# Half of the first output group's PSUM tiles move from ScalarE to VectorE, in a one-core hybrid decoder layer

## The chip, the cores and the metric

The kernel runs on one core of a Trainium2 chip. Its time is the device time of one execution in microseconds (us); the figure to be predicted is the median of a few executions. The core's engines are called PE (TensorE, the matrix products), DVE (VectorE), ACT (ScalarE), POOL (GpSimd) and SP (SyncE, which here only issues DMAs). Each engine works through its own list of instructions in order: an instruction that waits holds up everything behind it on its engine, and nothing on the others until they need its result.

## The reference

One layer of a decoder, sequence length 1024, model width 1024, all in float32:

```
x = x + 0.5 * swiglu(rms_norm(x))
x = x + concat(o_gdn, o_ssm) @ w_out      # the mixer
x = x + 0.5 * swiglu(rms_norm(x))
out = rms_norm(x)
```

The mixer projects the normalised input with one matrix and runs two kinds of heads over it. `o_gdn` comes from 8 heads of a gated delta rule (causal, in chunks, with a triangular solve in each chunk and a state that passes from chunk to chunk), each head normalised and gated. `o_ssm` comes from 16 state-space heads, gated by `silu(z)` and then normalised in two groups of 512 channels. The 2048 columns of both go through `w_out` (2048 x 1024). The normalisation of `o_ssm` is a factor for each token and group, so it can be applied after the product with `w_out`.

## The kernel before, in words

A matrix product in float32 precision is made of three passes: each operand is split into a high and a low part (`hi` by a ScalarE cast or scaling, `lo` by a VectorE subtraction), and `mm3` (lines 122 to 125) issues hi*hi, lo*hi and hi*lo, one product of 128x512 each. So a group of product rows in the profile always shows L123, L124 and L125 in turn.

The program runs in stages: first feed-forward block, gates and input projection, the state-space heads, the eight delta-rule heads, the output projection, second feed-forward block, final norm. The change touches the border between the last delta-rule head (head 7) and the output projection.

The output projection of the state-space part is cut into four groups (`n` = 0 to 3) of 256 columns of `o_ssm`. For each group `group_prep(n)` (line 1204) loads 256 rows of `w_out` and the group's slice of `o_ssm` by DMA, and splits both: `whi` (ACT, L138) and `wlo` (DVE, L139) are the weights, the tiles `mtt` (ACT, L1200 and DVE, L1201) the activations. `group_tile(n, b, dh)` (line 1211) then makes one output tile for token block `b` (0 to 7) and half `dh` (0 or 1) of the output columns: six products into one PSUM tile `ps_pj`, of which there are three in rotation. The tile is taken out of PSUM by one instruction: for group 0 a scaling that writes into the SBUF tile `xa` (L1220), for groups 1 to 3 a scaled addition onto `xa` on VectorE (L1222). Call the sixteen tiles of group 0 T0 to T15, in the order in which they are made: b = 0 with dh = 0, b = 0 with dh = 1, and so on. T0, T2, ... have dh = 0 and T1, T3, ... have dh = 1. The list `moved` holds their sixteen evictions, so `moved[4]` is that of T4 and `moved[5]` that of T5.

A tile's first product needs a free PSUM tile of the three, so T3 waits for the eviction of T0, T6 for T3 and so on.

Group 0 is made early: its operands come through other buffers (`out_start`, line 1228; there the weights are called `w`), and its tiles fill PE while heads 6 and 7 go through their serial parts. The serial parts that meet it are:

- head 6: its triangular solve, which runs from a chain of 62 small VectorE steps (`ft`, `fx`, L1496 and L1498) through DMAs, a VectorE transpose (`lv`, L1510) and small products with copies between them (L1516 to L1544), and then its recurrence over eight token blocks (L1554, L1556, L1559, L1561, L1565, L1568, L1573);
- head 7: `k_part` (line 1337) transposes the keys into two PSUM tiles `ps_mx` (L1346). For each of eight blocks ACT squares and sums a block (`jd`, L1350) and then DVE scales the same block (`kd`, L1352). Blocks of one PSUM tile take turns: each `kd` follows its `jd`, and the next `jd` follows that `kd`. When four blocks are read, the PSUM tile is free for the products of keys with keys and queries (`pg`, L1443 and L1444).

The order of instructions on each engine is set by a scheduler when the program is built. It ranks instructions by the order of the source and by its own estimate of when each could run. `with tc.issue_after(ins):` adds to that: instructions created inside the block on the engine of `ins` are queued behind `ins`. Line 1454 uses it to queue ACT's part of `group_prep(1)` behind T5's eviction. It binds only the engine on which that eviction runs.

Of the kernel before, what the change touches and what calls it, by code (L numbers as in the profile page):

```python
# [16 lines left out]
ALU = mybir.AluOpType  # L17
# [27 lines left out]
def kernel(  # L45
# [7 lines left out]
    V, A, G, T = nc.vector, nc.scalar, nc.gpsimd, nc.tensor  # L53
# [9 lines left out]
    def psum(tag):  # L63
        return ps.tile([P, 512], F32, name="ps_" + tag, tag=tag, bufs=PS_BUFS[tag])
# [57 lines left out]
    def mm3(o, wh, wl, mh, ml, first, last):  # L122
        T.matmul(o, lhsT=wh, rhs=mh, start=first, stop=False)  # L123
        T.matmul(o, lhsT=wh, rhs=ml, start=False, stop=False)  # L124
        return T.matmul(o, lhsT=wl, rhs=mh, start=False, stop=last)  # L125
# [759 lines left out]
    with tc.tile_pool(name="gtmp", bufs=1, side="right", reuse_waits="tile") as tp:  # L885
# [48 lines left out]
        for c in (15, 13, 11, 9, 7, 5, 3):  # L934
# [9 lines left out]
                               op0=ALU.mult, op1=ALU.mult)  # L944
# [259 lines left out]
    def group_prep(n):  # L1204

        w = load_rows_w(wp, w_out[0], (4 + n) * 256, "")
        m = out_bufs[1][n % 2 * 2:n % 2 * 2 + 2]
        ssm_prep(n, *m)
        return w, m

    def group_tile(n, b, dh, w, m):
        bs = slice(b * P, (b + 1) * P)
        ds = slice(dh * 512, (dh + 1) * 512)
        p = psum("pj")
        for j in range(2):
            last = mm3(p, m[0][:, j, bs], m[1][:, j, bs], w[0][:, j, ds], w[1][:, j, ds], j == 0, j == 1)
        o = out_bufs[0][b // 2][:, b % 2, ds]
        r = rstd_g[n // 2][:, b:b + 1]
        if n == 0:
            moved.append(A.mul(out=o, in_=p, mul=r))  # L1220
        else:
            V.scalar_tensor_tensor(out=o, in0=p, scalar=r, in1=o, op0=ALU.mult, op1=ALU.add)  # L1222
        return last

    FIRST_TILES = 4
    out_bufs, ready0, moved = [], [], []
# [107 lines left out]
    with ExitStack() as cg:  # L1334
# [37 lines left out]
        for h in range(GH):  # L1372
# [25 lines left out]
            else:  # L1398
# [15 lines left out]
                if h < GH - 1:  # L1414
                    conv_from(pre, 16 + h, vt_)
                    A.activation(out=zc, in_=zc, func=AF.Silu)
                    A.activation(out=vt_, in_=vt_, func=AF.Silu)
                else:
                    out_start()
                    for b in range(FIRST_TILES):  # L1420
                        for dh in range(2):
                            tile_end = group_tile(0, b, dh, *ready0[0])
                    tk, br2, kd = k_part(h, kt)
                    qe, dt = decays(h)
                    conv_from(pre, 16 + h, vt_)
                    A.activation(out=zc, in_=zc, func=AF.Silu)
                    A.activation(out=vt_, in_=vt_, func=AF.Silu)
# [9 lines left out]
            for b0 in range(0, NB, 2):  # L1437
# [8 lines left out]
                for i in range(2):  # L1446
                    V.scalar_tensor_tensor(out=u[:, b0 + i], in0=pg[:, i * 256:i * 256 + P],
                                           scalar=br2[:, b0 + i:b0 + i + 1], in1=dt[:, b0 + i],
                                           op0=ALU.mult, op1=ALU.mult)
                V.tensor_tensor(out=dt[:, b2],  # L1450
                                in0=pg.rearrange("p (i c) -> p i c", i=2)[:, :, P:2 * P],
                                in1=dt[:, b2], op=ALU.mult)
            if h == GH - 1:
                with tc.issue_after(moved[5].ins):
                    ready1 = group_prep(1)
            fs_u = dram.tile([4, NB, 32, 32], F32, name="fs_u", bufs=2)
            for j in range(4):
# [14 lines left out]
                            op0=ALU.mult, op1=ALU.add)  # L1472
# [20 lines left out]
            for j in range(31):  # L1493
                r, n = j // 4 + 1, 31 - j
# [46 lines left out]
            for b in range(NB):  # L1541
# [3 lines left out]
                            scalar1=-1.0, scalar2=None, op0=ALU.mult)  # L1545
# [90 lines left out]
    for n in range(4):  # L1636
        cur = ready
        for b in range(NB):

            if n == 0 and b < FIRST_TILES:  # L1640
                if b == 2:
                    ready = ready1
                continue
            if b == 2 and n < 3:
                ready = group_prep(n + 1)
                if n == 1:
                    loaded = out_load(0)
            elif b == 2:
                pair_prep(0, 0, ms[0], loaded)
                loaded = out_load(1)  # L1650
                wa = out_w(0, 0)
            for dh in range(2):
                group_tile(n, b, dh, *cur)
# [104 lines left out]
```

## Time and profile before

| | |
|---|---|
| median of 3 runs | 2297.78 us (2296.7 to 2298.23) |
| the profiled execution, its own time | 2296.6 us |
| its span, first to last instruction | 2294.9 us |
| granted TensorE clock over the span | 0.998 |
| busy: PE, DVE, ACT | 98%, 76%, 51% of the span |
| where the change lies | 1420 to 1600 us; the sixteen evictions L1220 start between 1423.4 and 1461.3 us |

In rows of the timeline the first number is the start in us from the beginning of the span, the second the length, then engine, line, operation, output<-inputs, shapes and how often; the bracket says how long the engine was idle before and whose end it waited for. Successive instructions of one engine overlap by about 0.1 us, so the distance between two starts is a little less than a length. In rows by windows the columns are the stretch, its length, and the busy time with the number of instructions of PE, PEld (weight loads), DVE, ACT and POOL, then the granted clock, the share of the DMA engines and GB/s. In rows of waits the numbers are the total in us, how often, and the longest.

### The profile page before, as it was taken

The page shows a single profiled execution, that of the slowest core. Times are in us where ns is not written, and L with a number is a line of the kernel's source. Part 1 is how long each engine was busy: PE and PEld are TensorE (multiplying, and loading weights), DVE is VectorE, ACT ScalarE, POOL GpSimd, SP SyncE. Part 2 cuts the span into 40 slices and gives each one's busy share as a digit, 9 for nine tenths or more (in the row PEclk, how much of TensorE's full clock was granted, in tenths as well). Part 3 has the DMA queues.
Part 4 walks back from the last instruction along what each step waited for, and adds up shares of the span by engine and source line. Part 5 has one row for each costly group of instructions (what it writes and reads, how often), then busy time and mean ns, then how long its engine had stood idle before and what let it go on. Part 6 is the DMA issues. An engine that isn't in the chain of part 4 may idle for free.

```text
span 2294.9 us, 31984 instructions
## 1 busy us (share of the span) xinstructions
PE 2257.9 (98%) x11654; PEld 1842.1 (80%) x11654; DVE 1751.5 (76%) x3225; ACT 1178.9 (51%) x2276; POOL 52.1 (2%) x118
## 2 busy tenths in 40 slices
PE   7999999999999999999999999999999999999998
PEld 5788888888878878888887777788878888888886
DVE  7989987769776887667667777778688676766787
ACT  7444433354366986875755566523543333334344
POOL 0000000000000110100000000000000000000000
PEclk9999999999999999999999999999999999999999
DMA  3467663497654433242356566436123232329446
GB/s 112 137 217 256 230 214 114 166 333 228 206 180 137 134 120 101 74 132 65 84 158 183 166 175 195 136 99 220 65 88 133 92 119 88 120 89 347 143 151 215
DMA packets 262194, 356.96 MB, mean 156 GB/s; under 512 B 60808, under 2 KB 167404, under 8 KB 260244
## 3 DMA queue, kind: packets, MB, share of 16 engines
q1 hardware_dynamic: 261220, 352.20, 47.2%
q0 software_dynamic: 816, 2.72, 0.3%
q8 instruction: 91, 1.49, 0.3%
q14 instruction: 67, 0.55, 0.1%
HBM read 249.34 MB, written 105.52 MB: 155 GB/s over the span
## 4 chain that ended last, share of the span: by engine, by line
PE 87%; ACT 6%; DVE 5%; issue 1%; DMA 1%; POOL 0%; SPq 0%; DVEq 0%; POOLq 0%; ACTq 0%
PE ps_pj L125 7%; PE ps_pj L123 7%; PE ps_pj L124 7%; PE ps_pj L335 6%; PE ps_pj L334 6%; PE ps_pj L336 6%; PE ps_mx L334 3%; PE ps_mx L336 3%; PE ps_mx L335 3%; PE ps_pj L564 2%; PE ps_pj L565 2%; PE ps_pj L563 2%; PE ps_pj L1260 2%; PE ps_oo L335 2%; PE ps_pj L1261 2%; PE ps_oo L334 2%
## 5 line engine op out<-in xcount | busy, mean ns | idle before, releaser
L336 PE MATMUL ps_pj<-bh,al 128*128 128x512 f32 x688 | 268.1, 390 | 0.0
L335 PE MATMUL ps_pj<-bl,ah 128*128 128x512 f32 x688 | 267.9, 389 | 0.0
L334 PE MATMUL ps_pj<-bh,ah 128*128 128x512 f32 x688 | 267.7, 390 | 0.0
L123 PE MATMUL ps_pj<-hhi,whi 128*128 128x512 f32 x576 | 229.4, 398 | 0.4 <-ACT gsb L901 0.4
L125 PE MATMUL ps_pj<-hhi,wlo 128*128 128x512 f32 x576 | 229.4, 398 | 0.0
L124 PE MATMUL ps_pj<-hlo,whi 128*128 128x512 f32 x576 | 228.3, 396 | 0.0
L336 PEld LDWEIGHTS ps_pj<-bh,al 128*128 128x128 f32 x688 | 129.2, 188 | 26.7
L335 PEld LDWEIGHTS ps_pj<-bl,ah 128*128 128x128 f32 x688 | 129.2, 188 | 26.6
L334 PEld LDWEIGHTS ps_pj<-bh,ah 128*128 128x128 f32 x688 | 129.0, 188 | 26.7
L317 DVE TENSOR_TENSOR as<-wst 128x512 f32<-128x512 f32 x220 | 144.3, 685 | 2.1 <-DMA wst<-in_ffn_w_up_dram 2.0
L241 ACT CAST hid<-hraw 128x1024 fp32r<-128x1024 f32 (+1 forms) x84 | 82.2, 980 | 123.9 <-PE ps_oo L565 46.3
L241 ACT CAST ah<-wst 128x512 fp32r<-128x512 f32 x88 | 54.5, 621 | 176.4 <-PE ps_oo L335 113.4
L242 DVE TENSOR_TENSOR al<-as,ah 128x512 fp32r<-128x512 f32 x220 | 141.1, 685 | 4.8 <-ACT ah L241 4.3
L334 PE MATMUL ps_mx<-bh,ah 128*128 128x512 f32 x352 | 138.6, 396 | 3.9 <-ACT m L343 1.3
L335 PE MATMUL ps_mx<-bl,ah 128*128 128x512 f32 x352 | 138.3, 393 | 0.5 <-DVE bl L242 0.5
L336 PE MATMUL ps_mx<-bh,al 128*128 128x512 f32 x352 | 137.8, 391 | 0.3 <-DVE al L242 0.3
L241 ACT CAST ah<-as 128x512 fp32r<-128x512 f32 x220 | 125.1, 618 | 24.1 <-DVE as L317 24.1
L125 PEld LDWEIGHTS ps_pj<-hhi,wlo 128*128 128x128 f32 x576 | 108.3, 188 | 21.9 <-issue 0.9
L123 PEld LDWEIGHTS ps_pj<-hhi,whi 128*128 128x128 f32 x576 | 108.4, 188 | 21.8 <-ACT gsb L901 0.8
L124 PEld LDWEIGHTS ps_pj<-hlo,whi 128*128 128x128 f32 x576 | 108.4, 188 | 21.1 <-issue 0.8
L242 DVE TENSOR_TENSOR hid<-hraw,hid 128x1024 fp32r<-128x1024 f32 (+1 forms) x84 | 95.0, 1131 | 26.3 <-ACT hid L241 26.1
L343 ACT COPY m<-ps_pj 128x512 f32<-128x512 f32 x88 | 51.4, 587 | 111.7 <-PE ps_pj L336 111.4
(505 smaller groups left out, 5635.4 us busy)
## 6 DMA issues: line engine op xcount, KB each, us to landing
hraw<-hid_scr SPq DMA_DIRECT2D x70, 512.0 KB, 3.9
wu_scr<-wunit SPq DMA_DIRECT2D x112, 256.0 KB, 3.6
wunits<-wu_scr SPq DMA_DIRECT2D x56, 512.0 KB, 3.8
hid_scr<-hs SPq DMA_DIRECT2D x110, 256.0 KB, 2.9
wst<-in_ffn_w_down_dram SPq DMA_DIRECT2D x50, 512.0 KB, 4.7
wst<-in_ffn_w_gate_dram SPq DMA_DIRECT2D x22, 1024.0 KB, 6.0
wst<-in_ffn_w_up_dram SPq DMA_DIRECT2D x22, 1024.0 KB, 6.0
hid_scr<-sg SPq DMA_DIRECT2D x44, 256.0 KB, 2.0
```

Source lines behind the costliest of these rows:

```text
L123: T.matmul(o, lhsT=wh, rhs=mh, start=first, stop=False)
L124: T.matmul(o, lhsT=wh, rhs=ml, start=False, stop=False)
L125: return T.matmul(o, lhsT=wl, rhs=mh, start=False, stop=last)
L241: return (A.copy(out=hi, in_=src), V.tensor_tensor(out=lo, in0=src, in1=hi.bitcast(F32), op=ALU.subtract))
L242: V.tensor_tensor(out=lo, in0=src, in1=hi.bitcast(F32), op=ALU.subtract))
L317: V.tensor_tensor(out=t, in0=v[0], in1=v[1], op=v[2])
L334: T.matmul(bank, lhsT=wh[:, k], rhs=bh[:, k], start=a, stop=False, skip_group_check=True)
L335: T.matmul(bank, lhsT=wh[:, k], rhs=bl[:, k], start=False, stop=False, skip_group_check=True)
L336: T.matmul(bank, lhsT=wl[:, k], rhs=bh[:, k], start=False, stop=z, skip_group_check=True)
L343: A.copy(out=t, in_=bank)
L563: T.matmul(bank, lhsT=hh, rhs=wh, start=first and k == 0, stop=False, skip_group_check=True)
L564: T.matmul(bank, lhsT=hh, rhs=wl, start=False, stop=False, skip_group_check=True)
```

## The change: eviction of T1, T3, ... by VectorE, and a second queueing rule

Two places change. In `group_tile` the eviction of group 0's tiles with dh = 1 is a VectorE scaling; those with dh = 0 stay on ScalarE. Where `group_prep(1)` is created, its ACT instructions are queued behind `moved[4]` (now the ACT one of the two) and its DVE instructions behind `moved[5]` (now on DVE). Before, only its ACT instructions were bound.

```diff
         if n == 0:
-            moved.append(A.mul(out=o, in_=p, mul=r))
+            if dh == 0:
+                moved.append(A.mul(out=o, in_=p, mul=r))
+            else:
+                moved.append(V.tensor_scalar(out=o, in0=p, scalar1=r, scalar2=None, op0=ALU.mult))
...
             if h == GH - 1:
-                with tc.issue_after(moved[5].ins):
+                with tc.issue_after(moved[4].ins), tc.issue_after(moved[5].ins):
                     ready1 = group_prep(1)
```

The scheduler also moves other instructions. In the changed program line numbers above 1220 are one to three higher (L1220 is L1221 on ACT and L1223 on DVE, L1352 is L1355, L1516 is L1519).

ACT, from T0's eviction (`xa`) to the second weight cast of group 1 (`whi`). Before:

```order
L1369 ACTIVATE dt<-dt,ngc 128x128 x2
L1426 ACT_TABLE_LOAD
L1426 ACTIVATE zc<-zc 128x1024
L1220 ACTIVATE xa<-ps_pj,rg_7158 128x512 x3
L1427 ACTIVATE vt__13312<-vt__13312 128x1024
L1220 ACTIVATE xa<-ps_pj,rg_7158 128x512
L138 CAST whi<-wst 128x1024
L1220 ACTIVATE xa<-ps_pj,rg_7158 128x512
L1350 ACTIVATE jd,tk<-ps_mx 128x128
L138 CAST whi<-wst 128x1024
```

The same place now:

```order
L1372 ACTIVATE dt<-dt,ngc 128x128 x6
L1221 ACTIVATE xa<-ps_pj,rg_7158 128x512
L1429 ACT_TABLE_LOAD
L1429 ACTIVATE zc<-zc 128x1024
L1221 ACTIVATE xa<-ps_pj,rg_7158 128x512
L138 CAST whi<-wst 128x1024
L1430 ACTIVATE vt__13312<-vt__13312 128x1024
L1221 ACTIVATE xa<-ps_pj,rg_7158 128x512
L138 CAST whi<-wst 128x1024
```

The table load now has two evictions ahead of it (T0, T2) where it had three; three evictions less stand between it and the second cast, and the first cast goes ahead of the `vt_` activation.

DVE, from the last step of head 6's chain (`fx`) to the transpose `lv`. Before:

```order
L1498 TENSOR_TENSOR fx<-fx,ft 128x8
L139 TENSOR_TENSOR wlo<-wst,whi 128x1024
L1352 TENSOR_SCALAR kd<-ps_mx,wend 128x128
L139 TENSOR_TENSOR wlo<-wst,whi 128x1024
L1352 TENSOR_SCALAR kd<-ps_mx,wend 128x128
L1201 SCALAR_TENSOR_TENSOR mtt<-nat,cols,mtt 128x1024
L1352 TENSOR_SCALAR kd<-ps_mx,wend 128x128
L1201 SCALAR_TENSOR_TENSOR mtt<-nat,cols,mtt 128x1024
L1352 TENSOR_SCALAR kd<-ps_mx,wend 128x128 x3
L1510 STREAM_TRANSPOSE lv<-lv 128x256
```

Now, from T7's eviction on:

```order
L1223 TENSOR_SCALAR xa<-ps_pj,rg_7158 128x512
L139 TENSOR_TENSOR wlo<-wst,whi 128x1024
L1355 TENSOR_SCALAR kd<-ps_mx,wend 128x128
L1201 SCALAR_TENSOR_TENSOR mtt<-nat,cols,mtt 128x1024
L1355 TENSOR_SCALAR kd<-ps_mx,wend 128x128
L1201 SCALAR_TENSOR_TENSOR mtt<-nat,cols,mtt 128x1024
L1355 TENSOR_SCALAR kd<-ps_mx,wend 128x128
L1223 TENSOR_SCALAR xa<-ps_pj,rg_7158 128x512
L1355 TENSOR_SCALAR kd<-ps_mx,wend 128x128 x2
L1223 TENSOR_SCALAR xa<-ps_pj,rg_7158 128x512
L1355 TENSOR_SCALAR kd<-ps_mx,wend 128x128 x2
L1513 STREAM_TRANSPOSE lv<-lv 128x256
```

The evictions of T9 and T11 now stand among the `kd` scalings, and seven of these instead of six come before the transpose.

PE, from the first key products (`ps_mx<-kt`) to the first product of the solve (L1516 before, L1519 now). Before, T11's first product is the one ahead of them:

```order
L123 MATMUL ps_pj<-w_13534,mtt 128x512
L1443 MATMUL ps_mx<-kt 128x128
L1444 MATMUL ps_mx<-qt,kt 128x128
L1443 MATMUL ps_mx<-kt 128x128
L1444 MATMUL ps_mx<-qt,kt 128x128
L124 MATMUL ps_pj<-w_13535,mtt 128x512
L125 MATMUL ps_pj<-w_13534,mtt 128x512
L123 MATMUL ps_pj<-w_13534,mtt 128x512
L124 MATMUL ps_pj<-w_13535,mtt 128x512
L1516 MATMUL ps_sc<-lv,u 32x32
```

Now it is T12's first product, and from the fourth key product on the list reads:

```order
L1447 MATMUL ps_mx<-qt,kt 128x128
L124 MATMUL ps_pj<-w_13535,mtt 128x512
L125 MATMUL ps_pj<-w_13534,mtt 128x512
L123 MATMUL ps_pj<-w_13534,mtt 128x512
L124 MATMUL ps_pj<-w_13535,mtt 128x512
L125 MATMUL ps_pj<-w_13534,mtt 128x512
L123 MATMUL ps_pj<-w_13534,mtt 128x512
L124 MATMUL ps_pj<-w_13535,mtt 128x512
L125 MATMUL ps_pj<-w_13534,mtt 128x512
L1519 MATMUL ps_sc<-lv,u 32x32
```

Ahead of the solve's first product PE now has fifteen products from T11 on (all of T11 and T12 and half of T13) where it had five.

## The prediction, made before the changed kernel ran

> **What bounds the kernel now.** First the page's head and its chain of waits.
>
> ```profile
> span 2294.9 us, 31984 instructions
> PE 2257.9 (98%) x11654; PEld 1842.1 (80%) x11654; DVE 1751.5 (76%) x3225; ACT 1178.9 (51%) x2276; POOL 52.1 (2%) x118
> PE 87%; ACT 6%; DVE 5%; issue 1%; DMA 1%; POOL 0%; SPq 0%; DVEq 0%; POOLq 0%; ACTq 0%
> ```
>
> PE is busy 98% of the span. The change adds and removes no product, so it can only win PE's idle time, and only where an eviction L1220 ends it. The windows of the stretch show how much that is.
>
> ```profile
> 1420.00:1430.00 10.00, 9.67 (x41) 6.91 (x40) 8.80 (x15) 9.03 (x17) 2.46 (x3) 1.00 0.39 142
> 1430.00:1440.00 10.00, 8.04 (x36) 6.30 (x37) 5.89 (x8) 10.00 (x22) 0.23 (x1) 1.00 0.41 92
> 1440.00:1450.00 10.00, 10.00 (x148) 7.97 (x148) 7.12 (x24) 7.56 (x17) 0.00 (x0) 1.00 0.60 213
> 1540.00:1550.00 10.00, 9.94 (x67) 8.37 (x67) 6.96 (x14) 5.97 (x16) 0.00 (x0) 1.00 0.01 2
> ```
>
> PE lacks 0.33 us in the first of these and 1.96 in the second; there ACT is busy for all 10 us and DVE for 5.89. From 1440 on PE is full. The waits of PE from 1400 to 1620 are a single row, and PE's timeline has its two places.
>
> ```profile
> PE ps_pj L123 <- ACT xa L1220: 2.3, 2, 2.0
> ...
> 1428.98 0.40 PE L125 MATMUL ps_pj<-w,mtt 128*128 128x512 f32 x1
> ...
> 1430.00 0.50 PE L123 MATMUL ps_pj<-w,mtt 128*128 128x512 f32 x1 [0.30 <-ACT xa L1220]
> ...
> 1433.37 0.48 PE L123 MATMUL ps_pj<-w,mtt 128*128 128x512 f32 x1
> ...
> 1437.43 0.39 PE L125 MATMUL ps_pj<-w,mtt 128*128 128x512 f32 x1
> 1439.78 0.50 PE L123 MATMUL ps_pj<-w,mtt 128*128 128x512 f32 x1 [1.96 <-ACT xa L1220]
> 1440.11 0.38 PE L1443 MATMUL ps_mx<-kt 128*128 128x128 f32 x2
> ```
>
> The first wait is T6's for T3's eviction; the second is T11's for T8's. Between 1433.37 and 1437.43 stand T8, T9 and T10 without a wait: 17 products on, 0.239 us apart, 1.43 for a tile of six. All that the change can remove by what it says is 0.30 + 1.96 = 2.26 us, 0.10% of the time. Two times closer than 0.2% (4.6 us) can't be told apart here, so I count all within 4.6 us as no change.
>
> **The change part by part.** Why T8's eviction is late is read from ACT's timeline.
>
> ```profile
> 1429.28 1.83 ACT L1220 ACTIVATE xa<-ps_pj,rg 128x512 f32<-128x512 f32 x3
> 1430.99 1.06 ACT L1427 ACTIVATE vt__13312<-vt__13312 128x1024 f32<-128x1024 f32 x1
> ...
> 1434.27 1.08 ACT L138 CAST whi<-wst 128x1024 fp32r<-128x1024 f32 x1
> ...
> 1435.47 2.22 ACT L1200 ACTIVATE mtt<-nat,cols 128x1024 fp32r<-128x1024 f32 x2
> ...
> 1437.80 1.09 ACT L1468 ACTIVATE qsq<-qt 128x1024 f32<-128x1024 f32 x1
> 1438.74 0.31 ACT L1350 ACTIVATE jd<-ps_mx 128x128 bf16<-128x128 f32 x1
> ...
> 1438.99 0.73 ACT L1220 ACTIVATE xa<-ps_pj,rg 128x512 f32<-128x512 f32 x1
> ```
>
> ACT works through a backlog: three evictions at a time (0.57 us apart: 1429.28 + 3 x 0.57 = 1430.99), activations, group 1's casts, then T8 at 1438.99, though T8's products were issued by 1433.37 + 1.43 = 1434.8.
>
> *The evictions that leave ACT.* Ahead of T8 stood T0 to T7; T1, T3, T5, T7 go. That is 4 x 0.57 = 2.3 us off ACT's queue before T8. One `jd` fewer stands ahead of T8 too (0.25, from 1438.74 to 1438.99), so if ACT stays busy T8 starts at 1438.99 - 2.3 - 0.25 = 1436.4 and PE may write T11 from about 1437.15. PE itself gets there when? Without the 0.30 at T6 it is that much earlier, and the transposes L1346 stand at one place instead of two (0.1): it comes to T11 at 1437.43 + 0.23 - 0.4 = 1437.25. So both waits go, with 0.1 to spare at the second.
>
> *The evictions that come to DVE.* No row has exactly this instruction. The nearest are a VectorE scaling out of PSUM with 512 elements for each of 64 partitions, the additions that evict the other groups, ScalarE's own evictions, and a scaling of 1024 elements from SBUF.
>
> ```profile
> L1544 DVE TENSOR_SCALAR u<-ps_sc x8: 681/682/683, 1071.3 to 1524.4; 64x512 f32<-64x512 f32 x8
> L1222 DVE SCALAR_TENSOR_TENSOR xa<-ps_pj,rg,xa x48: 714/746/751, 1462.8 to 1545.7; 128x512 f32<-128x512 f32 x48
> L1220 ACT ACTIVATE xa<-ps_pj,rg x16: 669/689/764, 1423.4 to 1461.3; 128x512 f32<-128x512 f32 x16
> L190 DVE TENSOR_SCALAR xt<-xt,rstd x6: 745/750/754, 32.8 to 1649.1; 128x1024 f32<-128x1024 f32 x6
> ```
>
> The bounds are half of L190's (0.37) and L1222's 0.75; I take L1544's 0.68, the same operation with the same source. The eight cost DVE 8 x 0.60 = 4.8 us of queue (0.08 overlaps), between 2.3 and 5.3 by the bounds. The Trainium skill, "VectorE: DVE Perf Modes", section "Why PSUM operands drop a tier", says that a PSUM operand holds float32 to one element a cycle where SBUF operands may go faster; by it L190's rate is out, and the eight cost 4.8 and not 2.3. That agrees with 682 ns for 512 elements here against 750 for 1024.
>
> What hides these 4.8 us? DVE's idle time of the stretch:
>
> ```profile
> 1423.44 1.27 DVE L847 SCALAR_TENSOR_TENSOR vt__13312<-pre,cols,vt__13312 128x1024 f32<-128x1024 f32 x1
> ...
> 1424.74 1.21 DVE L1433 TENSOR_TENSOR qe<-qe,qt 128x1024 f32<-128x1024 f32 x1
> ...
> 1433.60 1.23 DVE L139 TENSOR_TENSOR wlo<-wst,whi 128x1024 fp32r<-128x1024 f32 x1 [4.76 <-ACT whi L138]
> ...
> 1439.44 0.35 DVE L1352 TENSOR_SCALAR kd<-ps_mx,wend 128x128 f32<-128x128 f32 x1
> ...
> 1440.85 0.35 DVE L1352 TENSOR_SCALAR kd<-ps_mx,wend 128x128 f32<-128x128 f32 x1 [0.48 <-ACT jd L1350]
> 1441.12 0.43 DVE L1510 STREAM_TRANSPOSE lv<-lv 128x256 f32<-128x256 f32 x1
> ```
>
> DVE waits 4.76 us for group 1's first cast. T1, T3, T5 and T7 fall in or just ahead of it. T3, which PE now needs at 1429.21 for T6 (T5's last product 1428.98 + 0.23), stands behind two L847 (1.20 each), L1433 (1.13), T1 (0.60) and five small steps (0.1 each): 1423.44 + 2.40 + 1.13 + 0.60 + 0.5 = 1428.1, and it ends at 1428.75. That is 0.45 before PE asks.
>
> *The new queueing rule.* On ACT it binds the casts behind T4, on DVE the subtractions behind T5. Nobody waits for group 1's operands before PE is done with T15, whose eviction is the last start in L1220's row (1461.3), and both casts move ahead of 1434.27. I cost it at nothing; without that cover it would be one cast and one subtraction, 1.08 + 1.23 = 2.3 us.
>
> *T9 and T11 among the `kd`.* This is the part that can cost. Each `kd` alternates with a `jd` of ACT, so I followed both queues by hand, with the distances between starts above (0.60 for an eviction, 0.27 for a `kd`, 0.25 to 0.3 for a `jd`). After T8 (1436.5) and T10 (whose last product ends at 1437.4) ACT does the fourth `jd` by 1438.4, DVE, with T9 done at 1438.0, the fourth `kd` by 1438.8. PE needs that for L1443, which follows T12's first product, at 1437.25 + 1.43 + 0.33 = 1439.0: 0.2 to spare. T11 comes out at 1439.0 to 1439.6; then `kd`, `jd`, `kd`, and the transpose L1510 at 1440.75 to 1441.2, near its old place. PE wants it at about 1441.8, as it now has T12's rest and half of T13 first. At L1516 PE stood at
>
> ```profile
> 1442.03 0.21 PE L1516 MATMUL ps_sc<-lv,u 32*32 32x32 f32 x1
> ```
>
> and it now comes there some 0.2 us earlier with ten more products done (five from T11 on before, fifteen now): 0.2 + 10 x 0.239 = 2.6 us ahead, at most; the waits alone are 2.26. I take 2.5.
>
> *Behind L1516.* More handovers follow in head 6's solve, with copies on ACT such as
>
> ```profile
> 1441.58 0.41 ACT L1528 COPY lv<-lv 32x256 f32<-32x256 f32 x1
> ...
> 1447.05 0.58 ACT L1539 COPY lv<-ps_sc 64x512 f32<-64x512 f32 x1
> ```
>
> By the same following they have little slack: ACT's L1530 now stands behind T12's eviction (0.25 to spare), L1542 waits for L1532, now queued behind the copy L1539 (none to spare), L1559 for L1544 (0.1), and ACT's second recurrence scaling behind group 2's first L1200, which needs T15's first half (none). I take off 0.1 to 0.15 for each, 0.5 in all.
>
> *Sum.* -2.5 + 0.5 = -2.0 us against the profiled execution, which took 2296.6 (span 2294.9 and 1.7 around it): 2294.6. The median of the runs is 2297.78, 1.2 above that execution, so the median should be near 2297.78 - 2.0 = 2295.8.
>
> **The rivals.**
>
> *A. The wait changes its name (2297.8).* PE's next need after T11 is the freed key bank. Were the `jd` and `kd` to keep their old times (the fourth `kd` at 1439.44), PE would stop at L1443 or L1516 for nearly what it stood at T11. For it: slack of 0.2 us. Against it: ACT, which sets the `jd`, is the engine that is relieved, and DVE had 0.48 us idle even among the `kd`. It gives -2.26 + 2.3, no change.
>
> *B. VectorE's and ScalarE's evictions hold up the solve (2299.4).* T11 waits for PE on DVE with the transpose L1510 behind it, T12 does so on ACT with L1528, L1529 and L1530 behind it. Suppose PE comes to them one tile (1.43 us) later against these queues than I followed. Then L1516 waits 1.43 - 0.6 = 0.8 us, L1537 waits for T12 and three small copies (0.6 + 3 x 0.4 = 1.8), and L1542 for L1539 and L1532 (0.6 + 0.4 = 1.0): 3.6 - 2.0 = 1.6 slower. It decides where PE is over 0.6 us late at T11. An eviction of over 1.2 us on DVE instead of 0.68 would use up the same slack; against that, no row of DVE on 512 elements in PSUM exceeds 0.751, and it has 0.02 of this rival's 0.09. The Trainium skill, "Advanced Engine Details and Errata", section "The Read-Write Bubble", points to this last case: it advises the opposite of this change, since ScalarE is closer to PSUM and VectorE to SBUF. The rows don't bear it out here (682 to 746 ns on DVE, 689 on ACT).
>
> *C. The recurrences pay at each block (2306.3).* The sixteen blocks' steps of heads 6 and 7 pass through DVE, and the re-sorted queue puts an L1222 or L1201 ahead of `sn` or `rr` in other places. If that eviction came first each time and PE had only its usual three products (3 x 0.239 = 0.7 us) to cover, each of 14 `sn` would cost up to 0.75: 10.5 - 2.0 = 8.5 slower.
>
> ```profile
> L1556 DVE SCALAR_TENSOR_TENSOR rr<-ps_sc,negeg,vr 128x128 f32<-128x128 f32 x16 | 5.6, 348 | 3.9 <-PE ps_sc L1554 3.9
> ...
> L1573 DVE SCALAR_TENSOR_TENSOR sn<-sn,egt,ps_sc 128x128 f32<-128x128 f32 x14 | 4.8, 346 | 5.8 <-PE ps_sc L1568 5.7
> ```
>
> Against: in these rows it is DVE that waits for PE, 3.9 and 5.8 us, not the other way, with 48 evictions L1222 in the same queue already, and the windows show PE full there. It decides where a step comes more than 0.7 us after its products.
>
> *D. More is won than PE's wait (2292.5).* The windows leave 0.06 us of idle elsewhere in the stretch, so over 4.6 us could only come from a stage that isn't touched.
>
> **How the numbers follow.** Forecast (stall gone, 1.5 to 2.6 us won) 0.63; A 0.20; B 0.09; C 0.05; D 0.03. The time is the forecast's, 2295.8. The low end is 2.6 us won and the 1.1 by which the lowest run lay under the median: 2297.78 - 3.7 = 2294.1. The high end takes in A with the highest run (2298.2) and B's 2299.4, and leaves out C and D. Only D is faster by over 4.6 us (0.03); C is slower by more (0.05); the forecast, A and B lie within, 0.92.
>
> **What the changed profile would show.** Right: no row "PE <- ACT xa" or "<- DVE xa" above 0.5 us, T8's eviction near 1436.5, DVE's idle of 4.76 before the first `wlo` gone, window 1430 to 1440 with PE at 9.7 or more. A: PE idle at L1446 or L1519 (the old L1443, L1516) of 1 us and more, released by `kd` or `lv`. B: PE idle at L1540, L1545 or L1562 (old L1537, L1542, L1559). C: idle at the recurrence's products from 1450 on. Evictions on DVE outside 0.6 to 0.76 us would prove the price wrong, and a difference over 4.6 us with PE's idle time unchanged would prove the whole reading wrong.

## The result, and the profile after

The changed kernel was timed in 21 executions, and so was the kernel before beside it. The medians are 2294.31 us (lowest to highest 2292.81 to 2297.40) and 2297.99 us (2296.29 to 2300.97); the ratio is 0.9982 with a 95% interval of 0.9977 to 0.9988, that is 2.8 to 5.3 us less. The profiled execution took 2294.78 us. The forecast was 2295.8 in a range of 2294.1 to 2299.4: the time is inside the range, at its low end. The prediction had counted everything within 0.2% (4.6 us) as no change, with 0.92; the 0.18% lie inside that bound, but these runs tell them from no change clearly.

The page's head and chain of the changed kernel:

```profile
span 2293.1 us, 31979 instructions
...
PE 2256.5 (98%) x11654; PEld 1840.6 (80%) x11654; DVE 1756.8 (77%) x3233; ACT 1174.5 (51%) x2268; POOL 52.8 (2%) x118
...
PE 83%; DVE 7%; ACT 5%; DMA 3%; issue 1%; POOL 0%; SPq 0%; DVEq 0%; ACTq 0%; POOLq 0%
```

Eight instructions have changed sides: 3225 to 3233 on DVE, 2276 to 2268 on ACT. PE's products are the same 11654. The windows of the stretch:

```profile
1420.00:1430.00 10.00, 9.93 (x42) 7.39 (x41) 10.00 (x18) 9.00 (x16) 1.84 (x1) 1.00 0.58 209
1430.00:1440.00 10.00, 10.00 (x48) 7.90 (x47) 9.53 (x15) 9.87 (x18) 0.86 (x2) 1.00 0.37 86
1440.00:1450.00 10.00, 10.00 (x140) 8.16 (x138) 7.17 (x24) 4.61 (x18) 0.00 (x0) 1.00 0.61 218
```

PE is full where it lacked 1.96 us, and DVE has gone from 5.89 to 9.53 us in the middle window: its idle time is used. Among the waits of PE between 1400 and 1620 the row "PE ps_pj L123 <- ACT xa L1220: 2.3" is gone, and no other has come in its place. The two groups of evictions, and the places in ACT's and DVE's timelines that the prediction spoke of:

```profile
L1221 ACT ACTIVATE xa<-ps_pj,rg x8: 668/682/703, 1425.5 to 1455.5; 128x512 f32<-128x512 f32 x8
...
L1223 DVE TENSOR_SCALAR xa<-ps_pj,rg x8: 732/738/751, 1426.8 to 1458.5; 128x512 f32<-128x512 f32 x8
```

```profile
1438.33 0.28 ACT L1353 ACTIVATE jd<-ps_mx 128x128 bf16<-128x128 f32 x1
...
1438.57 1.53 ACT L1221 ACTIVATE xa<-ps_pj,rg 128x512 f32<-128x512 f32 x2
```

```profile
1430.08 0.73 DVE L1223 TENSOR_SCALAR xa<-ps_pj,rg 128x512 f32<-128x512 f32 x1
...
1432.67 1.21 DVE L139 TENSOR_TENSOR wlo<-wst,whi 128x1024 fp32r<-128x1024 f32 x1
...
1439.41 0.74 DVE L1223 TENSOR_SCALAR xa<-ps_pj,rg 128x512 f32<-128x512 f32 x1
1440.39 0.75 DVE L1355 TENSOR_SCALAR kd<-ps_mx,wend 128x128 f32<-128x128 f32 x2 [0.24 <-ACT jd L1353]
1441.06 0.74 DVE L1223 TENSOR_SCALAR xa<-ps_pj,rg 128x512 f32<-128x512 f32 x1
...
1442.76 0.43 DVE L1513 STREAM_TRANSPOSE lv<-lv 128x256 f32<-128x256 f32 x1
```

To lay these times beside those of before, the two profiles need a common mark. Three places of PE's timeline serve: T0's first product, the first product of the second feed-forward stage behind its wait, and that stage's first product into `ps_pj`. Before:

```profile
1420.20 0.40 PE L123 MATMUL ps_pj<-w,mtt 128*128 128x512 f32 x1
...
1679.40 0.74 PE L334 MATMUL ps_sc<-bh,ah 128*128 128x512 f32 x2 [1.35 <-ACT bh L241]
...
1685.59 0.39 PE L334 MATMUL ps_pj<-bh,ah 128*128 128x512 f32 x1
```

After:

```profile
1422.26 0.40 PE L123 MATMUL ps_pj<-w,mtt 128*128 128x512 f32 x1
...
1679.20 0.73 PE L334 MATMUL ps_sc<-bh,ah 128*128 128x512 f32 x2 [1.36 <-ACT bh L241]
...
1683.82 0.39 PE L334 MATMUL ps_pj<-bh,ah 128*128 128x512 f32 x1
```

The profile after reaches T0 2.06 us later, in code that is the same in both (so far do two executions differ). Part of it is PE's wait for `xtb` (L218, near 643 us), which comes out between nothing and 1.7 us from profile to profile: 1.0 in this one, no row of it in that of before. From T0 to the feed-forward stage it needs 256.94 us instead of 259.20: 2.26 less, as much as the two waits. And then, in a stage that isn't touched, it wins another 1.57 us in six (4.62 against 6.19). That last number was in no term of the sum. Where it comes from is the main thing that the experiments show.

### The profile page after: what moved, and what is told of

Same layout as the page of the kernel before. It is cut to its first block, busy times and chain, and to the rows that moved or that the text cites. A ratio compares the mean times of both kernels' runs of the same rounds, so it can differ in the third digit from the quotient of the medians.

```text
span 2293.1 us, 31979 instructions
## 1 busy us (share of the span) xinstructions
PE 2256.5 (98%) x11654; PEld 1840.6 (80%) x11654; DVE 1756.8 (77%) x3233; ACT 1174.5 (51%) x2268; POOL 52.8 (2%) x118
## 4 chain that ended last, share of the span: by engine, by line
PE 83%; DVE 7%; ACT 5%; DMA 3%; issue 1%; POOL 0%; SPq 0%; DVEq 0%; ACTq 0%; POOLq 0%
PE ps_pj L123 7%; PE ps_pj L125 7%; PE ps_pj L124 7%; PE ps_pj L334 6%; PE ps_pj L335 6%; PE ps_pj L336 6%; PE ps_mx L334 3%; PE ps_mx L336 3%; PE ps_mx L335 3%; PE ps_oo L335 2%; PE ps_oo L334 2%; PE ps_oo L336 2%; PE ps_pj L564 2%; PE ps_pj L1263 2%; PE ps_pj L1265 2%; PE ps_pj L1264 2%
## 5 line engine op out<-in xcount | busy, mean ns | idle before, releaser
L123 PE MATMUL ps_pj<-hhi,whi 128*128 128x512 f32 x576 | 229.2, 398 | 0.4 <-ACT gsb L901 0.4
L123 PEld LDWEIGHTS ps_pj<-hhi,whi 128*128 128x128 f32 x576 | 108.3, 188 | 21.8 <-ACT gsb L901 0.8
```

## The experiments

Two theories were set against each other. **C, the granted clock:** a wait of PE of about 2 us costs its own length, and in part of the executions also some 1.5 us more, because the granted clock is halved behind it. **N, chance:** the wait costs its length alone, and what the 21 runs show beyond 2.3 us is scatter. Each run lists its mean granted clock to three decimals. The clock is also halved for some 4 to 7 us at the span's end, where PE has little left to do, so the third decimal counts the losses only roughly: 0.999 is mostly a run with no halved stretch behind a wait, 0.998 one with one, 0.997 one with two. The table holds all timed runs (mean of the runs; ratio to the kernel before on the same chip, with its 95% interval).

| kernel | runs | mean us | 0.999 | 0.998 | 0.997 and less | ratio |
|---|---|---|---|---|---|---|
| before, beside the experiments | 98 | 2299.1 | 9 | 40 | 49 | 1 |
| after, first measurement | 21 | 2294.6 | 12 | 9 | 0 | 0.9982 (0.9977 to 0.9988) |
| q1: the queueing rule alone | 11 | 2298.1 | 0 | 6 | 5 | 0.9993 (0.9984 to 1.0002) |
| f0: before, second stage filled | 11 | 2296.8 | 8 | 3 | 0 | 0.9987 (0.9978 to 0.9995) |
| f1: after, second stage filled | 11 | 2294.8 | 10 | 1 | 0 | 0.9977 (0.9968 to 0.9986) |
| g1: before, T10 twice | 11 | 2297.6 | 5 | 6 | 0 | 0.9988 (0.9979 to 0.9997) |
| a1: after once more | 12 | 2294.2 | 10 | 2 | 0 | 0.9978 (0.9970 to 0.9987) |
| p2: T5 and T7 alone | 12 | 2295.7 | 8 | 4 | 0 | 0.9988 (0.9980 to 0.9997) |
| v16: all sixteen on VectorE | 12 | 2302.1 | 0 | 1 | 11 | 1.0014 (1.0005 to 1.0024) |
| d2: T9 and T11 evicted twice | 10 | 2293.9 | 6 | 3 | 1 | 0.9980 (0.9971 to 0.9989) |
| g2: before, both places filled | 11 | 2297.0 | 11 | 0 | 0 | 0.9994 (0.9985 to 1.0003) |
| f4: after, second stage filled with four | 11 | 2294.8 | 11 | 0 | 0 | 0.9984 (0.9975 to 0.9993) |
| h1: T1, T3, T5, T7 alone | 11 | 2293.6 | 8 | 3 | 0 | 0.9977 (0.9968 to 0.9986) |
| s1: the split alone | 11 | 2295.5 | 2 | 9 | 0 | 0.9985 (0.9976 to 0.9994) |

### q1: the queueing rule alone, which is the kernel before again

```diff
-                with tc.issue_after(moved[5].ins):
+                with tc.issue_after(moved[4].ins), tc.issue_after(moved[5].ins):
```

> All evictions of the first group stay on ScalarE; only the queueing rule of the second group's operands is the new one (behind T4 and T5). Built so, every engine's instructions stand as in the kernel before, so this is the kernel before once more, and shows how far two sets of its runs and two of its profiles differ. Both theories: same as before within 0.3 us in the mean of the runs (2298.3), PE's waits of 0.30 and 1.96 us at T6 and T11 there again. Theory C (the granted clock): an idle time of PE of about 2 us halves the granted clock for about 3 us in part of the executions, at 1.6 us each; this kernel has two such places (T11's wait, and the 1.35 + 0.55 us ahead of the second feed-forward stage at 1678), so most runs' mean clock is 0.998 or lower, against 12 of 21 at 0.999 after the change. Theory N (chance): clocks as after the change, 0.999 in over half of the runs.

The mean is 2298.12 and no run reaches 0.999; five have 0.997. The kernel before, timed beside it, had a mean of 2299.9, so two sets of runs of one program can lie 1.8 us apart, with an interval of the ratio that holds 1. The profile is worth more than the time. PE's wait for `xa` is the same as before, but here the windows show the granted clock (the column behind POOL's) at one half behind T11's wait:

```profile
1440.02:1443.43 3.41, 1.46 (x10) 1.38 (x11) 2.69 (x7) 3.41 (x12) 0.00 (x0) 1.00 0.54 68
1443.43:1446.84 3.41, 3.41 (x38) 2.42 (x37) 1.52 (x4) 1.81 (x8) 0.00 (x0) 0.50 0.98 402
1682.35:1685.76 3.41, 2.15 (x8) 1.44 (x9) 3.31 (x7) 1.86 (x3) 0.00 (x0) 1.00 1.07 354
```

In the profile of the kernel before it is the other way round, full clock at T11 and half behind the second feed-forward stage's wait:

```profile
1435.80:1439.21 3.41, 2.02 (x9) 1.31 (x7) 3.41 (x5) 3.41 (x8) 0.00 (x0) 1.00 0.38 58
1678.16:1681.57 3.41, 1.62 (x6) 1.06 (x7) 3.34 (x6) 1.42 (x3) 0.00 (x0) 1.00 1.03 350
1681.57:1684.98 3.41, 3.41 (x10) 2.63 (x9) 3.29 (x6) 2.03 (x4) 0.00 (x0) 0.50 0.72 238
```

Two executions of one program, and product for product q1 loses 1.43 us between 1441 and 1444 of before's clock and wins 1.5 back at 1682 to 1685. The windows are cut where the clock changes: both halved stretches last 3.41 us. So T11's wait of 1.96 us has a second price. It is paid in the executions in which the wait falls whole, or nearly so, into one such step of 3.41 us, as in q1, where PE is idle for 1.95 of it; in the profile of before the edge of a step cuts the wait (1.39 idle in the first part), and nothing happens.

### f0, f1 and f4: the second stage's wait filled with work that is thrown away

Products ahead of that stage's first own product, in its own PSUM tile, which then starts anew (`fills` is `[[], [range(6)]]`, in f4 `range(4)`):

```diff
+        for k in fill and fill.pop(): T.matmul(bank, lhsT=st[7][0][:, k % 4], rhs=H[7][0][:, k % 4], start=k == 0, stop=k == 5, skip_group_check=True)
...
-            open_bank(H, st, "c1", 1, None, "sc")
+            open_bank(H, st, "c1", 1, None, "sc", fill)
```

f0, on the kernel before:

> The kernel before, with six more products (0.23 us each, 1.4 us) put ahead of the second feed-forward stage's wait of 1.35 us; their sums are thrown away. PE is then not idle there for more than about 0.6 us. Theory C: the window 1680 to 1685 shows a clock of 1.00 in every profile, and the mean of the runs falls by 0.5 to 1.0 us (1.6 us in a third to two thirds of the executions), to about 2297.5. Theory N: no drop is saved that matters; 0 to 0.2 us slower, 2298.3 to 2298.5.

Eight of 11 runs at 0.999, where the kernel before has 9 of 98; the mean is 2296.84, 1.3 us under q1's and 3.1 under the kernel before beside it, and the profile has no halved step. As C expected, and more than the 0.5 to 1.0 that it named.

f1, on the changed kernel:

> The changed kernel with the same six products ahead of the second feed-forward stage's wait. Theory C: no place with about 2 us of idle time is left but the end, so nearly all runs have a mean clock of 0.999 and lie near the 2293.9 us that the changed kernel's runs at 0.999 have (mean over the runs now 2294.6): 0.7 us faster than the changed kernel, 4.4 faster than before. Theory N: 2294.6 to 2294.8, clocks mixed as they were.

The clock is as C said (10 of 11). The time is not: 2294.82, where 2293.9 was expected, no less than the changed kernel's.

f4, the same with four products:

> The changed kernel with four thrown-away products ahead of the second feed-forward stage (0.9 of its wait of 1.35 us, so that they delay nothing, where six ended 0.2 us late). Theory C: nearly all runs at a mean clock of 0.999, about 0.5 us (a third of the executions by 1.6 us) below the changed kernel: near 2294.0, 4 to 4.5 us faster than before; the fastest version of all. Theory N: as the changed kernel, clocks mixed, 2294.5.

All 11 runs at 0.999, and 2294.76: again no gain over the changed kernel that the runs could show. The intervals are 2 us to either side, four times the 0.5 that was looked for, so a gain of that size is neither shown nor excluded.

### g1 and g2: T11's wait filled in the kernel before

T10's six products made twice, so that PE works while T8's eviction is awaited:

```diff
-        for j in range(2):
+        for j in (0, 1, 0, 1) if n == 0 and (b, dh) == (5, 0) else (0, 1):
```

> The kernel before, with the six products of the eleventh tile (T10) made twice, the second time from the start again: 1.43 us of PE work put into the wait of 1.96 us that stands behind it, of which 0.5 to 0.7 us is left. T8's eviction, for which T11 waits, is not touched. Theory C: the wait of T11 itself lowers the clock in part of the executions of the kernel before; with PE busy in it that goes, and the mean of the runs falls by 0.5 to 1.0 us to about 2297.5 though PE has more to do. Theory N (the stall costs its 1.96 us and nothing else): 0 to 0.3 us slower than before, 2298.3 to 2298.6.

T11's first product in PE's timeline of g1:

```profile
1440.25 0.50 PE L123 MATMUL ps_pj<-w,mtt 128*128 128x512 f32 x1 [0.56 <-ACT xa L1220]
```

It starts when T8's eviction lets it, as ever; only the idle time ahead of it is shorter. The mean is 2297.57, 0.55 under q1's and 2.3 under the kernel before beside it, with five of 11 runs at 0.999. More work, no less waiting for T8, and rather less time; against q1, the same program as before, the step is too small for certainty by the times alone.

g2 has this filling and f0's:

> The kernel before with both fillings: T10's products made twice ahead of T11's wait, and six thrown-away products ahead of the second feed-forward stage. In the profiles so far the granted clock changes only on a grid of 3.41 us, and it was halved behind each grid step in which PE was idle for 1.79 us or more (1.79, 1.91, 1.96) and behind none with 1.63 or less (1.63, 1.59, 1.54, 1.40), the solve's small products apart. Theory C: no grid step is left with more than 1.3 us of idle time, so nearly every run has a mean clock of 0.999, and the time is that of the kernel before at 0.999, about 2296, though both stalls are still paid (2 to 2.5 us over the changed kernel with its wait filled, below). Theory N: clocks as in the kernel before (0.998 and 0.997 in 9 of 10 runs), time 2298.3 or more.

This settles the clock: 11 of 11 runs at 0.999. The 9 of 98 of the kernel before become all, by nothing but keeping PE at work in two waits. The time (2297.02 median, 2297.04 mean) is a good microsecond over the 2296 expected. By the third decimal neither g2 nor f4 has a halved step in any run, so the two side by side give the price of the waits alone: 2297.04 - 2294.76 = 2.3 us, with a 95% interval of some 1.4 to 3.1. The rows say 2.26.

The profiles say the same without the scatter of what runs ahead of T0. The first and the last of the three places, in f0 and then in f1:

```profile
1422.26 0.40 PE L123 MATMUL ps_pj<-w,mtt 128*128 128x512 f32 x1
...
1686.13 0.39 PE L334 MATMUL ps_pj<-bh,ah 128*128 128x512 f32 x1
```

```profile
1423.37 0.40 PE L123 MATMUL ps_pj<-w,mtt 128*128 128x512 f32 x1
...
1684.95 0.39 PE L334 MATMUL ps_pj<-bh,ah 128*128 128x512 f32 x1
```

Between the two places f0 needs 263.87 us and f1 261.58: 2.29 for the waits, with no halved step in either. Unfilled, the changed kernel needs 261.56 too, but the kernel before needs 265.39 (265.32 in q1): 1.5 more than f0, for one halved step, wherever it falls.

### a1: the changed kernel again

> The changed kernel once more, beside the next three. Theory C (the removed wait was worth its own 2.3 us, and besides the drop of the granted clock that it brought in part of the executions): 3 to 4.4 us faster than before, mean clock 0.999 in about half of the runs and never two drops (0.997); before has 0.998 and 0.997 in nearly all. Theory N (only the wait, the rest was chance): 2.0 to 2.6 us faster.

Ratio 0.9978, means 2294.22 against 2298.62: 4.4 us. C's range. Over both measurements 22 of 33 runs of the changed kernel are at 0.999 and none is at 0.997.

### p2, h1 and s1: parts of the change

p2, with T5 and T7 alone on VectorE (`if dh == 0 or b not in (2, 3):`):

> Only T5 and T7 go to VectorE, the other fourteen evictions stay on ScalarE. The queue's sum says: six evictions and three of the small steps stand ahead of T8 on ScalarE, against eight and four before, so T8 starts 2 x 0.57 + 0.25 = 1.4 us earlier and T11's wait falls from 1.96 to about 0.6 us; T6's wait of 0.30 for T3 stays. 1.4 us faster than before by the waits alone. Theory C: a wait of 0.6 us is too short to lower the clock, so the other drop alone is left and the sum is 2 to 2.8 us faster. Rival (the wait is set by something else than the number of evictions ahead, ScalarE's casts for one): T11 waits over 1.3 us, under 1 us faster.

ACT's and PE's timelines of p2:

```profile
1439.24 0.71 ACT L1221 ACTIVATE xa<-ps_pj,rg 128x512 f32<-128x512 f32 x1
```

```profile
1431.63 0.50 PE L123 MATMUL ps_pj<-w,mtt 128*128 128x512 f32 x1 [0.30 <-ACT xa L1221]
1440.00 0.50 PE L123 MATMUL ps_pj<-w,mtt 128*128 128x512 f32 x1 [0.56 <-ACT xa L1221]
```

T6's wait stays at 0.30 and T11's falls to 0.56, where the sum gave 1.96 - 1.39 = 0.57. T11's wait is set by what stands ahead of T8 on ScalarE, one by one. The ratio is 0.9988, 2.8 us, of which the waits are 1.4 (0.8 in the profile from T0 to the second feed-forward stage: 258.39 against 259.20). The wait of 0.56 halved no clock in this profile, and 8 of 12 runs are at 0.999.

h1, with the first four alone (`if dh == 0 or b >= 4:`):

> Of the eight evictions only T1, T3, T5 and T7 go to VectorE, those that stood ahead of T8 on ScalarE; T9, T11, T13 and T15 stay there. The queue's sum puts T8 where the changed kernel has it (1436.5 on the clock of before), so T6 and T11 wait for nothing and the time is the changed kernel's within 0.5 us; the four later ones bring nothing of their own. Rival (ScalarE's later handovers, the copies of head 6's solve behind T11 and T13, come late without the four): PE waits 0.5 us and more at the solve or the first recurrences, 0.5 to 1.5 us slower than the changed kernel.

No wait of PE for `xa` is left, and the ratio is 0.9977. The whole gain is in T1, T3, T5 and T7; the four later ones bring nothing that the runs can tell. The profiles rather say that they cost something: from T0 to the second feed-forward stage h1 needs 255.41 us and the changed kernel 256.94, though PE is idle for 1.7 to 1.8 of it in both. With the four moved as well, the scheduler puts PE's products in another order, and they keep PE busy for 1.4 us more (255.12 against 253.71). Why that order is dearer was not followed up.

s1, the split with the old rule:

```diff
-                with tc.issue_after(moved[4].ins), tc.issue_after(moved[5].ins):
+                with tc.issue_after(moved[5].ins):
```

> The eviction is split as in the changed kernel, but the queueing rule of the second group's operands is the old one (behind T5 alone, which is now on VectorE). Built so, TensorE's, VectorE's and SyncE's queues are the changed kernel's; on ScalarE one of the two casts moves ahead of T0 and six other steps, to the place ahead of five evictions. All theories expect T6's and T11's waits gone. If the rule matters, T0 to T3 come 1.05 us later and PE waits at T4 to T6 for up to 1 us; if the backlog on ScalarE is gone with the split alone, the time is the changed kernel's within 0.4 us.

No row of PE's waits in the stretch, and 256.68 us from T0 to the second feed-forward stage against 256.94: the rule does not matter there. The ratio 0.9985 agrees with the changed kernel's; 9 of the 11 runs are at 0.998, more than the third seen elsewhere, and its profile shows why a run is: the second stage's wait, in a step with 1.72 us idle (3.41 - 1.69).

```profile
1675.23:1678.64 3.41, 1.69 (x7) 0.75 (x5) 3.34 (x6) 1.69 (x3) 0.00 (x0) 1.00 0.91 281
1678.64:1682.05 3.41, 3.23 (x8) 2.56 (x9) 3.26 (x6) 1.99 (x5) 0.00 (x0) 0.50 1.00 328
```

### d2: VectorE's price doubled among the small steps

```diff
-                moved.append(V.tensor_scalar(out=o, in0=p, scalar1=r, scalar2=None, op0=ALU.mult))
+                moved.append([V.tensor_scalar(out=o, in0=p, scalar1=r, scalar2=None, op0=ALU.mult) for _ in range(2 if b in (4, 5) else 1)][-1])
```

> The changed kernel, with T9 and T11 each evicted twice on VectorE (the same values again), 0.6 us more at each of the two places between the small steps of head 6. By the slack that the prediction counted (0.2 us at the fourth small step, 0.6 at the transpose ahead of the solve, 0.1 to 0.25 and none behind it) PE waits 0.4 us at the key products or the solve, and 0.4 to 1.2 us are lost against the changed kernel. Rival (the slack was counted too thin, as the changed kernel's stretch that won 2.5 us instead of 2.0 hints): PE shows no new wait over 0.3 us and the time is that of the changed kernel within 0.3 us.

The rival was right: no wait of PE in the stretch, mean 2293.90. It is not a clean test of the slack, because the scheduler answers the longer queue: it puts two more products ahead of the solve's first and others between its steps. What it shows is that, as this program is built, 0.7 us more at either place is absorbed.

### v16: all sixteen on VectorE

`if dh == 0:` becomes `if False:`. T4's eviction is then on VectorE too, so the rule no longer binds ScalarE's part of `group_prep(1)`; this was not tried apart.

> All sixteen tiles of the first group are taken out by VectorE. It has 4.8 us more to do than in the changed kernel, and the idle time of 4.76 us that hid the first eight is used up. The theory of the cover: T3 stands behind T0 to T2 and is late for T6 by 0.5 to 1 us, and the small steps and T8 to T11 follow late; PE waits 1.5 to 4 us in the stretch, so the time is 1 to 4 us over the changed kernel's. Rival (VectorE has more slack than the queue shows, its evictions are hidden anyway): within 0.5 us of the changed kernel.

The cover is used up, as expected, and PE waits:

```profile
PE ps_mx L1446 <- DVE kd L1355: 1.4, 1, 1.4
PE ps_sc L1519 <- DVE lv L1513: 0.6, 1, 0.6
PE ps_sc L1540 <- ACT lv L1533: 0.6, 1, 0.6
PE ps_pj L123 <- DVE xa L1223: 0.2, 1, 0.2
```

That is 2.8 us, in the range of 1 to 4. But the kernel is 7.8 us over a1 (2302.05 against 2294.22), and the rest is the clock again, here for three steps in a row:

```profile
1437.50:1440.91 3.41, 2.19 (x42) 1.85 (x42) 3.38 (x8) 1.57 (x6) 0.00 (x0) 1.00 0.99 330
1440.91:1444.32 3.41, 3.41 (x53) 2.10 (x52) 2.48 (x7) 0.82 (x4) 0.00 (x0) 0.50 0.65 271
1444.32:1447.73 3.41, 3.41 (x22) 2.88 (x22) 2.60 (x7) 1.36 (x3) 0.00 (x0) 0.50 0.02 5
1447.73:1451.15 3.42, 3.42 (x18) 2.67 (x18) 0.00 (x0) 1.58 (x3) 0.00 (x0) 0.50 0.00 0
```

Three steps at some 1.5 us are 4.5, and 2.8 + 4.5 = 7.3. The profile bears this out: between the same two places as in f0 and f1 it needs 268.82 us, 7.26 more than the changed kernel. Theory and rival were both too small, by the same term as the prediction.

## Why the prediction was right and wrong

*What bounds the kernel* was right: the change could only win where an eviction ended PE's idle time, and both places are gone.

*T8's eviction* was put at 1436.4 on the clock of before. It starts at 1438.57, and 2.06 less is 1436.5. p2 shows the same arithmetic for half the change.

*The price on VectorE* was taken as 0.68 in bounds of 0.37 to 0.75; it is 0.738. ScalarE's own took 0.682 (medians): VectorE is 8% dearer from PSUM here, and that is hidden. *T3* was to end 0.45 us before PE asks; it ends at 1430.81, and T6's first product starts at 1431.31 in PE's timeline, 0.5 later.

*T9, T11 and the small steps:* T9 ends at 1440.15 (1438.1 on the clock of before, forecast 1438.0), T11 starts at 1441.06 (1439.0, forecast 1439.0), the transpose at 1442.76 (1440.7, forecast 1440.75 to 1441.2). PE's timeline has the first L1446 at 1441.07, which is 1439.0, and the first L1519 at 1443.93, 0.7 us behind the transpose's end. All as followed by hand.

*The new queueing rule*, costed at nothing, costs and brings nothing that s1 could show (q1, the same program as before, says nothing of it).

**First failing step, the sum: "-2.5 + 0.5 = -2.0".** The 2.5 was right: PE's first L1519 stands at 1443.93 - 2.06 = 1441.87, 0.16 us ahead of the old place with ten more products done, 0.16 + 10 x 0.239 = 2.55. The 0.5 for thin handovers behind it was mis-sized: at the second feed-forward stage 2.26 of the 2.55 are left, so 0.3 went, and at no handover, since no wait of PE stands there. With the clock kept full in both kernels the runs give 2.3. The queue followed by hand said "none to spare"; the deduction made of that a loss, though nothing had shown PE arriving first. This step is worth 0.3 of the 1.7 us between the forecast's 2.0 and the 3.7 by which the medians differ.

**Second failing step, and the larger, the bound: "All that the change can remove by what it says is 0.30 + 1.96 = 2.26 us".** A wait of PE also has a price in the clock, which the sum put at nothing, and the rows quoted for it (PEclk 1.00 in all four windows) came from an execution in which T11's wait happened not to pay it. In the profile of before it was paid elsewhere, at 1681.57, where it did not look like part of the change. How much this is over many executions can be estimated from the table. Of the 98 runs of the kernel before that were timed beside the experiments, by the third decimal, 9 had no halved step, 40 had one and 37 two, that is 1.33 for each of these 86; of the changed kernel's 33 runs 22 had none and 11 one, 0.33. One step fewer, at 1.45 us, and 2.3 for the waits make 3.7 to 3.8. The other 12 runs of the kernel before, with a mean clock of 0.995 and less (mean 2303.6, 5.1 us over the mean of the 86; none of the changed kernel's 33 runs is so low), add 12/98 x 5.1 = 0.6 to the difference of the means, which over all runs is 4.6 (2299.1 against 2294.5).

Two things in this estimate are only argued. That the 12 runs are T11's wait followed by several halved steps, as in v16: no profile caught one. And that the one step fewer is T11's alone: if every place of a step's edge were equally likely, at least 1.7 us of that wait (the limit, below) would fall into one step for (3.41 - 1.96 + 2 x 0.26) / 3.41 = 58% of the places, 0.8 us on average and not 1.45. f0, where T11's wait alone was left, had a halved step in 3 of 11 runs, and g1, where the second stage's was left, in 6 of 11.

**Third, the yardstick:** "Two times closer than 0.2% (4.6 us) can't be told apart". With 21 runs of each the interval was 0.055% to either side. "No change" with 0.92 rested on a coarser measurement than was made.

*The rivals:* A (the wait changes its name) and B (the solve held up) fell: no row of PE's waits in the stretch. B's last case, a dearer eviction on VectorE, fell with 0.738 and with d2. C (the recurrences pay) did not happen. D, more than PE's wait won, came in, with about 1.4 of the 3.7 us, if not with the 5.3 that it named; its reason, that more "could only come from a stage that isn't touched", described the profile pair (1.57 us at 1680) and missed that the touched stage has the same price to pay.

## What to carry to other kernels

Price a wait of the busiest engine twice: its length, and what the clock does behind it; two waits of 2.26 us together cost 2.3 in this kernel where the clock held, and 3.7 by the medians of the first measurement. One profile shows one draw of that, so compare the mean clock of many runs before calling a difference chance. And when an eviction can be moved to an engine that sits idle just there, count what stands ahead of the one that is waited for: four of the eight moved evictions were the whole gain.

## What the runs showed of the hardware

**In this kernel the clock changes in steps of 3.41 us, and half a step of PE's idle time halves it in the next one.** In before, q1, g1 and s1 the halved stretch is 3.41 us long, in v16 10.24, three of them. Where the steps lie differs from execution to execution. The Trainium skill, "TensorE: Matmul & The Clock Gate", section "What's actually happening", tells of a free-running window of 3413 ns; the traces agree, with 3.41. The same page's section "HAM oscillation — how this bites in real kernels" gives as the rule no idle gaps of PE above some 3.4 us. Here that is too lenient. The steps with the most idle time, in d2, f1 and p2, with the clock full in the step that follows:

```profile
1674.58:1677.99 3.41, 1.84 (x7) 0.86 (x6) 3.34 (x6) 1.54 (x3) 0.00 (x0) 1.00 0.88 274
1677.99:1681.40 3.41, 3.08 (x13) 2.52 (x14) 3.25 (x6) 1.99 (x5) 0.00 (x0) 1.00 1.00 322
```

```profile
643.23:646.64 3.41, 1.78 (x9) 1.17 (x8) 3.29 (x8) 3.41 (x5) 0.00 (x0) 1.00 1.00 368
646.64:650.05 3.41, 3.33 (x18) 2.66 (x19) 3.41 (x5) 2.50 (x4) 0.00 (x0) 1.00 0.38 114
```

```profile
1679.25:1682.66 3.41, 1.91 (x7) 1.30 (x8) 3.34 (x6) 1.71 (x3) 0.00 (x0) 1.00 1.07 361
1682.66:1686.07 3.41, 3.41 (x17) 2.71 (x16) 3.28 (x7) 1.75 (x4) 0.00 (x0) 1.00 0.60 193
```

Idle for 1.57, 1.63 and 1.50 us, the next step ran at full clock; idle for 1.72 (s1), 1.79 (before), 1.91 (g1: 3.41 - 1.50) and 1.95 (q1) it was halved. Among these the limit lies between 1.63 and 1.72, about half of a step, and the idle time need not be in one piece: the second stage's is 1.35 and 0.55 with products between.

**Not settled:** v16 lost the clock behind a step with only 1.22 us idle (3.41 - 2.19), filled with the solve's 32x32 products; perhaps small products count for less, but that was not tried alone. And the filled kernels' runs at 0.999 (f0 2296.5, g2 2297.0) lie 0.7 to 1.2 us over the nine of the kernel before at 0.999 (2295.9), f1's and f4's some 0.8 over the changed kernel's. In f1's profile 0.1 us of that stands behind T0 (T0 to PE's last product takes 862.11 us, in the changed kernel 861.98), in f4's 0.5. f1's T0 itself comes late, in code that is the same in all: it starts at 1423.37, in the changed kernel at 1422.26 and in a1 at 1419.99, with 1.6, 1.0 and 0.2 us of waiting for `xtb` ahead. Whether that is so over many runs is open.
